# Score and value products of neighbouring maps issued in turns on the two halves of the tensor engine

## The chip, the cores and the metric

The kernel runs on one core of a Trainium2 chip. The metric is the device time of one execution in microseconds (us). A core has a tensor engine that does matrix products (PE; PEld is its weight load), a vector engine (DVE), a scalar engine (ACT), a general engine (POOL), and a sync engine (SP) whose queue starts most DMA transfers. All products here are fp32 or split fp32r; a plain fp32 product shows in the trace as two PE instructions.

## The reference

Two transformer blocks on 256 tokens of width 1024. The first mixes a gated delta rule (4 heads of 128, chunks of 64, a triangular solve) with a sliding "dilated" softmax attention (8 heads of 64), then has a dense gated feed-forward layer. The second has two layers, each with an attention and a mixture of 16 experts (top 2 of one group of 4). Layer one's attention is differential: 8 heads, each with two softmax maps of head size 64,

```
s = einsum('bqhmd,bkhmd->bmhqk', qb, k) + bias
p = softmax(where(allowed, s, NEG_INF))
a = p[:, 0] - lam_full * p[:, 1]
o = einsum('bhqk,bkhe->bqhe', a, v)
```

Layer two's attention is chunked: 16 heads of 64, one map each. So there are 8 + 16 + 16 = 40 maps of 256 queries by 256 keys. All are causal by blocks of 128: queries 128 to 255 see all 256 keys, queries 0 to 127 only the first 128.

## The kernel before, in words

**Layout.** The queries and keys of two heads (or of the two maps of one differential head) lie one above the other in the partitions: the tile `qT[:, blk, :]` has the features of one in partitions 0 to 63 and of the other in 64 to 127. A score product contracts over 64 partitions and so uses half of the rows of the tensor engine; the other half is free for the other map. A value product of `plain_heads` has 64 value features as stationary columns and contracts over 128 keys; it uses half of the columns, and writes its head's half of the partitions of the result.

**One map.** `scores` takes one PSUM tile and makes two products into it (lines 631 and 632, four PE instructions), then a fused add and minimum on DVE for each of the two query blocks (634, 636), two exponentials with sums on ACT (638, 639), and a reciprocal (640). The caller scales the rows (664, 665). `flip` transposes the map by three PE transposes (645 to 647) and copies it out (224 or 230, ACT and DVE in turns). `pv` makes the two value products of a head (653, 654, four PE instructions). After the odd head `split` writes the two halves of an fp32r number (ACT, then DVE, line 234).

**Stages and order.** `plain_heads` runs its heads through `lag`: step i issues the scores of head i, the flip of head i-2 and the value products of head i-3. It is used in three places: for the 8 dilated heads, whose steps `fill` drops between the steps of the delta rule (145 to 182 us of the span), and for four groups of 4 chunked heads (820 to 905 us). `diff_heads` does the same for the 8 differential heads, both maps of a head in one step (460 to 515 us). In the two attentions `weave` issues the steps of the first heads between the projections of the second half (`half(1)`, lines 586 to 588), and the steps of the later heads between the output projection (`proj(0)`, the same lines). The framework's planner takes the instructions in this order and sets the order on each engine by their readiness under its own costs, unless a line keeps them in program order. On the chip every engine takes its instructions in that order.

**Slots.** PSUM tiles of `ps` come from four slots (`pb`) and four more (`pa`, accumulators). SBUF tiles of `w2` (ten slots) hold the maps, the flipped maps and, in `half(1)`, the squares and normalised rows of the queries and keys (`unit_rows`). The expert weights are loaded by SP into ring slots and into tiles that the attention gives back (`wpair`, line 295; `v` among them).

Of the kernel before, what the change touches and what calls it, by code (L numbers as in the profile page):

```python
# [170 lines left out]
def tile_block(ctx: ExitStack, tc: tile.TileContext, a: dict, out: bass.AP, dbg=None):  # L171
# [11 lines left out]
    mm = nc.tensor.matmul  # L183
# [15 lines left out]
    def w2(shape, name, dt=F32):  # L199
        return act.tile([128] + shape, dt, tag="w2", name=name, bufs=10)  # L200
# [4 lines left out]
    def s1(w, name, bufs=2):  # L205
        return sm.tile([128, w], F32, tag=name, name=name, bufs=bufs)

    def ps(n=512, tag="pb"):
        p = pa if tag == "pa" else pb
        return p.tile([128, n], F32, tag=tag, name=tag)  # L210
# [21 lines left out]
    def split(h, l, i, eng=None):  # L232

        return A_.copy(h, i), (eng or V).tensor_tensor(l, i, h.bitcast(F32), op=ALU.subtract)  # L234

    def split_scaled(h, l, i, scale):
        return (A_.activation(h, i, AF.Copy, scale=scale),
                V.scalar_tensor_tensor(l, i, scale, h.bitcast(F32), op0=ALU.mult, op1=ALU.subtract))
# [231 lines left out]
    def rsq(o, i, scale):  # L470

        A_.activation(o, i, AF.Ln, bias=epsc, scale=scale)
        A_.activation(o, o, AF.Exp, scale=-0.5)
# [58 lines left out]
    def spread(rs):  # L532

        r = w2([S], "rows")
        for b in range(T):
            p = ps(128, "pa")
            mm(p, rs[:, b:b + 1].to_broadcast([128, 128]), ident, start=True, stop=True)
            V.tensor_copy(r[:, b * 128:(b + 1) * 128], p)
        return r
# [77 lines left out]
    def lag(n, *stages):  # L617

        for i in range(n + len(stages) - 1):
            for j, f in enumerate(stages):  # L620
                if 0 <= i - j < n:
                    f(i - j)
            yield


    def scores(qT, kT, blk, half, nbias, pt, den):


        h0 = half * 64
        p = ps(384)  # L630
        mm(p[:, 0:256], qT[h0:h0 + 64, blk, 128:256], kT[h0:h0 + 64, blk, :], start=True, stop=True)
        mm(p[:, 256:384], qT[h0:h0 + 64, blk, 0:128], kT[h0:h0 + 64, blk, 0:128], start=True, stop=True)
        mn = s1(2, "mn", 4)
        V.tensor_tensor_reduce(out=pt[:, 0:256], in0=p[:, 0:256], in1=nbias[:, ::-1], scale=1.0, scalar=3e38,
                               op0=ALU.add, op1=ALU.min, accum_out=mn[:, 0:1])
        V.tensor_tensor_reduce(out=pt[:, 256:384], in0=p[:, 256:384], in1=nbias[:, 0:128][:, ::-1], scale=1.0, scalar=3e38,
                               op0=ALU.add, op1=ALU.min, accum_out=mn[:, 1:2])
        A_.activation(pt[:, 0:256], pt[:, 0:256], AF.Exp, bias=mn[:, 0:1], scale=-1.0, accum_out=den[:, 0:1])
        A_.activation(pt[:, 256:384], pt[:, 256:384], AF.Exp, bias=mn[:, 1:2], scale=-1.0, accum_out=den[:, 1:2])
        V.reciprocal(den, den)  # L640

    def flip(pt):

        p = ps(384)
        nc.tensor.transpose(p[:, 0:128], pt[:, 256:384], ident)
        nc.tensor.transpose(p[:, 128:256], pt[:, 0:128], ident)
        nc.tensor.transpose(p[:, 256:384], pt[:, 128:256], ident)
        t = w2([384], "ptT")
        evac(t, p)
        return t  # L650

    def pv(o, v0, v1, t):
        mm(o, v0, t[:, 0:256], start=True, stop=False)
        mm(o[:, 128:256], v1, t[:, 256:384], start=False, stop=True)

    def plain_heads(h0, n, qT, kT, v, nbias, y):

        pts, ts, os_ = {}, {}, {}

        def first(i):  # L660
            h = h0 + i
            pt, den = w2([384], "pt"), s1(2, "den", 4)
            scores(qT, kT, h // 2, h % 2, nbias(h), pt, den)
            V.tensor_scalar(pt[:, 0:256], pt[:, 0:256], den[:, 0:1], None, op0=ALU.mult)
            V.tensor_scalar(pt[:, 256:384], pt[:, 256:384], den[:, 1:2], None, op0=ALU.mult)
            pts[h] = pt

        def second(i):
            ts[h0 + i] = flip(pts.pop(h0 + i))

        def third(i):
            h = h0 + i
            if h % 2 == 0:
                os_[h // 2] = ps(256)
            o = os_[h // 2]
            pv(o[h % 2 * 64:h % 2 * 64 + 64, :], v[:, 0, h * 64:h * 64 + 64], v[:, 1, h * 64:h * 64 + 64], ts.pop(h))
            if h % 2:
                split(*y(h // 2), o)

        return lag(n, first, lambda i: None, second, third)  # L680

# [18 lines left out]
    def l2(shape, name):  # L700
        return l1p.tile([128] + shape, F32, tag="l2", name=name, bufs=5)
# [29 lines left out]
    y = [None, None]  # L731
# [20 lines left out]
    n = 0  # L752
# [64 lines left out]
    for u in range(6):  # L817
        for j, (wh, wl) in enumerate(subs(a["w_qkv"][u] if u else first_)):
            f = 2 * u + j
            p = ps(256, "pa")  # L820
            feat(p, hh, wh, wl)
            o = qkvT[f // 4][:, f % 4]
# [17 lines left out]
        if u % 2:  # L840
            o = qkvT[u // 2].rearrange("p f t -> p (f t)")
# [13 lines left out]
    for h in range(4):  # L855
# [5 lines left out]
        p = ps(512)  # L861
        mm(p, ones, sq.rearrange("p i t -> p (i t)"), start=True, stop=True)
        r = w2([2, S], "rsq")
# [7 lines left out]
    def k_(h, b):  # L871
        return kq[:, h, b, 0, :]

    def q_(h, b):
        return kq[:, h, b, 1, :]
# [4 lines left out]
    p = ps(512)  # L880
# [25 lines left out]
    for b in range(T):  # L906
        for h2 in range(2):
            p = ps(512).rearrange("p (h i t) -> p h i t", h=2, i=2)
            for i in range(2):
                h = 2 * h2 + i  # L910
                mm(p[:, i].rearrange("p i t -> p (i t)"), k_(h, b), kq[:, h, b].rearrange("p i t -> p (i t)"),
                   start=True, stop=True)
# [7 lines left out]
    for b in range(T):  # L920
        p = ps(512)
# [6 lines left out]
    p = ps(512)  # L928
# [7 lines left out]
    for lv in range(6):  # L936
        os_ = w2([8, 64], "os")
# [20 lines left out]
        n = 128 if lv < 5 else 64  # L958
# [20 lines left out]
    u0, S1, r1, v1 = (l2([4, 128], n) for n in ("u0", "S1", "r1", "v1"))  # L979
    oo = l4([T, 512], "oo")  # L980

    def four(f):
        p = ps(512)
        for h in range(4):
            lhsT, rhs = f(h)
            mm(p[:, h * 128:(h + 1) * 128], lhsT, rhs, start=True, stop=True)
        return p
# [8 lines left out]
    p = four(lambda h: (k_(h, 1), S1[:, h]))  # L996
# [3 lines left out]
    p = four(lambda h: (q_(h, 1), S1[:, h]))  # L1000
    for h in range(4):
        o = oo[:, 1, h * 128:(h + 1) * 128]
        evac(o, p[:, h * 128:(h + 1) * 128], eg[:, 4 + h:5 + h])
    evac(flat(v1), four(lambda h: (YF[:, 4 + h], r1[:, h])))
    p = four(lambda h: (aq[:, 4 + h], v1[:, h]))
# [18 lines left out]
    for b in range(T):  # L1024
        for h in range(4):
            o = oo[:, b, h * 128:(h + 1) * 128]
            V.scalar_tensor_tensor(o, o, rso[:, b * 4 + h:b * 4 + h + 1], sz[:, b, h * 128:(h + 1) * 128],
                                   op0=ALU.mult, op1=ALU.mult)
    for h2 in range(2):
        p = ps(512).rearrange("p (h t) -> p h t", h=2)  # L1030
# [43 lines left out]
    nb = []  # L1074
# [20 lines left out]
    for f in range(NFF):  # L1095
        rooms[0] = "s8" if 1 <= f < 21 else "s"
        p, pu = ps(S), ps(S)
        for q, (wh, wl) in zip((p, pu), subs(a["w_gu"][f], by=(V, G) if f == 0 else None, behind=cols_done if f in (1,) else None)):
            feat(q, hh, wh, wl)
        o = w2([S], "gate")  # L1100
# [62 lines left out]
    h = cols_split(tx, spread(rs[:, 2:4]), mod[0]["gs1"], mod[0]["sh1"])  # L1163
# [463 lines left out]
    def diff_heads(c, qT, kT, v, y):  # L1627
        pts, ts, ons = {}, {}, {}

        def first(i):  # L1630
            h = 4 * c + i
            ab, dens = [], []
            for j in range(2):
                pt, den = w2([384], "pt"), s1(2, "den", 4)
                scores(qT, kT, h, j, nb[c][:, i, :], pt, den)
                ab.append(pt)
                dens.append(den)
            V.tensor_scalar(dens[1], dens[1], nlam, None, op0=ALU.mult)
            for j, sl in enumerate((slice(0, 256), slice(256, 384))):
                V.tensor_scalar(ab[1][:, sl], ab[1][:, sl], dens[1][:, j:j + 1], None, op0=ALU.mult)  # L1640
                V.scalar_tensor_tensor(ab[0][:, sl], ab[0][:, sl], dens[0][:, j:j + 1], ab[1][:, sl],
                                       op0=ALU.mult, op1=ALU.add)
            pts[i] = ab[0]

        def second(i):
            ts[i] = flip(pts.pop(i))

        def third(i):
            h = 4 * c + i
            t = ts.pop(i)  # L1650
            o = ps(256).rearrange("p (b d) -> p b d", b=2)
            v0, v1 = v[:, 0, h * 128:(h + 1) * 128], v[:, 1, h * 128:(h + 1) * 128]
            mm(o[:, 0], t[:, 0:128], v0, start=True, stop=True)
            mm(o[:, 1], t[:, 128:256], v0, start=True, stop=False)
            mm(o[:, 1], t[:, 256:384], v1, start=False, stop=True)
            on, ss = w2([T, 128], "on"), s1(2, "oss", 4)
            for b in range(T):
                A_.activation(on[:, b], o[:, b], AF.Square, accum_out=ss[:, b:b + 1])
            rsq(ss, ss, 1.0 / 128)
            V.tensor_tensor(on, o, ss.unsqueeze(2).to_broadcast([128, T, 128]), op=ALU.mult)  # L1660
            ons[i] = on

        def fourth(i):
            on = ons.pop(i)
            p = ps(256)
            for b in range(T):
                nc.tensor.transpose(p[:, b * 128:(b + 1) * 128], on[:, b], ident)
            split_scaled(y[0][c][:, i], y[1][c][:, i], p, sub8)

        return lag(4, first, second, third, fourth)  # L1670

    def between():
# [21 lines left out]
    h = cols_split(tx[0], kept(spread(rs), 1), m_["gs1"], m_["sh1"])  # L1694

    nb = []
# [41 lines left out]
```

## Time and profile before

| | before |
|---|---|
| median of 3 runs | 1158.78 us (1157.76 to 1162.37) |
| profiled execution | 1160.73 us, span 1158.7 us |
| PE busy | 1103.9 us (95%) |
| PE weight load busy | 710.5 us (61%) |
| DVE busy | 595.2 us (51%) |
| ACT busy | 449.6 us (39%) |
| mean granted PE clock | 0.984 |
| DMA | 349.71 MB, mean 302 GB/s |

A matrix product's time in a row is from its start to its modelled end, and successive products overlap; the time that a product costs the engine is the distance from its start to the next one's. A row of the timeline merges successive products of one line: its start is the start of the first.

### The profile page before, as it was taken

What the parts mean: (1) busy time and instruction counts of PE and PEld (TensorE: products, weight loads), DVE (VectorE), ACT (ScalarE), POOL (GpSimd) and SP (SyncE); (2) the same over time, 40 slices, a digit from 0 to 9 for tenths busy, and PEclk for the clock granted to TensorE, in tenths of its full rate; (3) what the DMA queues carried; (4) which work ended last, traced back from release to release, by engine and by line L of the source; (5) the groups of instructions that cost most, each with busy time, mean ns of one, the idle gap of its engine ahead of it and who ended that gap; (6) DMA issues with size and microseconds to landing.
All of it is one profiled execution on the core that took longest, in us unless ns stands there. A gap on an engine that the chain in (4) does not pass through costs nothing. (4 is left out here: it accounts for less than half of the span.)

```text
span 1158.7 us, 16795 instructions
## 1 busy us (share of the span) xinstructions
PE 1103.9 (95%) x6524; PEld 710.5 (61%) x6524; DVE 595.2 (51%) x1211; ACT 449.6 (39%) x907; POOL 161.3 (14%) x132
## 2 busy tenths in 40 slices
PE   8999999999999989998999997999999899999798
PEld 6967766799898968785443433337776544343332
DVE  6954355798999666886231212126566713121212
ACT  5752254656555465775111102026555511110200
POOL 2223112132223141012000000003221100000000
PEclk9999999999999989999999999999999989999999
DMA  8686777878887945357798999997663779899994
GB/s 326 224 314 227 294 263 242 293 254 330 323 319 284 370 149 188 128 210 257 298 383 327 424 424 420 422 420 272 202 194 133 267 278 384 339 424 424 422 420 198
DMA packets 53007, 349.71 MB, mean 302 GB/s; under 512 B 6356, under 2 KB 7108, under 8 KB 12984
## 3 DMA queue, kind: packets, MB, share of 16 engines
q1 hardware_dynamic: 50288, 342.51, 75.9%
q0 software_dynamic: 1792, 5.62, 1.8%
q8 instruction: 54, 0.88, 0.3%
q10 hardware_dynamic: 840, 0.43, 0.1%
q14 instruction: 33, 0.27, 0.1%
HBM read 347.40 MB, written 1.14 MB: 301 GB/s over the span
## 5 line engine op out<-in xcount | busy, mean ns | idle before, releaser
L1571 PE MATMUL pb<-w,XT 128*64 128x512 f32 x864 | 200.4, 613 | 10.1 <-PEq L1531 10.1
L234 ACT CAST wh<-w 128x1024 fp32r<-128x1024 f32 x132 | 137.7, 1044 | 100.8 <-PE pa L587 74.0
L234 DVE TENSOR_TENSOR wl<-w,wh 128x1024 fp32r<-128x1024 f32 x110 | 135.2, 1230 | 58.5 <-ACT wh L234 49.5
L1571 PEld LDWEIGHTS pb<-w,XT 128*64 128x64 f32 x864 | 61.7, 140 | 127.8 <-issue 123.3
L1608 PE MATMUL pb<-w,heT 128*64 128x512 f32 x480 | 108.1, 596 | 1.5 <-ACT heT L224 1.5
L1590 DVE TENSOR_TENSOR he<-he,pb 128x512 f32<-128x512 f32 (+1 forms) x20 | 11.4, 581 | 175.4 <-PE pb L1571 175.4
L586 PE MATMUL pa<-wh,hh 128*128 128x512 f32 x224 | 91.6, 410 | 2.5 <-ACT hh L559 2.5
L587 PE MATMUL pa<-wh,hl 128*128 128x512 f32 x224 | 89.7, 400 | 3.0 <-POOL hl L557 1.7
L1589 ACT ACTIVATE he<-pb 128x512 f32<-128x512 f32 (+1 forms) x20 | 10.0, 512 | 207.7 <-PE pb L1571 207.7
L588 PE MATMUL pa<-wl,hh 128*128 128x512 f32 x224 | 89.3, 399 | 0.0
L234 POOL TENSOR_TENSOR wl<-w,wh 128x1024 fp32r<-128x1024 f32 x22 | 53.0, 2408 | 248.5 <-ACT wh L234 197.2
L1611 DVE SCALAR_TENSOR_TENSOR he<-pb,gsl,g 128x512 f32<-128x512 f32 x32 | 24.0, 751 | 96.9 <-PE pb L1608 96.8
L1608 PEld LDWEIGHTS pb<-w,heT 128*64 128x64 f32 x480 | 32.7, 137 | 64.6 <-issue 58.6
L570 PE MATMUL pb<-hh,whl 128*128 128x256 f32 x320 | 61.9, 286 | 0.0
L383 POOL TENSOR_TENSOR acc<-acc,wa 128x512 f32<-128x512 f32 x24 | 41.4, 1724 | 125.9 <-DVE acc L385 90.9
L234 ACT CAST yh<-he 128x512 fp32r<-128x512 f32 x30 | 18.5, 617 | 103.6 <-DVE he L1611 103.6
L570 PE MATMUL pb<-hh,wh 128*128 128x256 f32 x192 | 54.4, 284 | 0.0
L570 PE MATMUL pb<-hl,wh 128*128 128x256 f32 x192 | 54.3, 283 | 0.0
L570 PE MATMUL pb<-hh,wl 128*128 128x256 f32 x192 | 54.3, 283 | 0.0
L570 PEld LDWEIGHTS pb<-hh,whl 128*128 128x128 f32 x320 | 51.2, 191 | 2.3 <-issue 1.8
L587 PEld LDWEIGHTS pa<-wh,hl 128*128 128x128 f32 x224 | 43.3, 193 | 12.5 <-DVE hl L560 2.2
L586 PEld LDWEIGHTS pa<-wh,hh 128*128 128x128 f32 x224 | 42.8, 192 | 12.8 <-ACT hh L559 3.4
(459 smaller groups left out, 2317.5 us busy)
## 6 DMA issues: line engine op xcount, KB each, us to landing
w<-in_m_gu SPq DMA_DIRECT2D x108, 1024.0 KB, 10.8
w<-in_m_dn SPq DMA_DIRECT2D x58, 1024.0 KB, 9.0
wa<-in_ada_p SPq DMA_DIRECT2D x24, 1024.0 KB, 5.0
wa<-in_ada_w SPq DMA_DIRECT2D x24, 1024.0 KB, 5.0
w<-in_w_gu SPq DMA_DIRECT2D x22, 1024.0 KB, 6.9
w<-in_a_qkv SPq DMA_DIRECT2D x12, 1024.0 KB, 12.4
wx<-in_m_gu SPq DMA_DIRECT2D x12, 1024.0 KB, 5.9
w<-in_b_qkv SPq DMA_DIRECT2D x12, 1024.0 KB, 14.8
```

The lines of the kernel that those rows point to most:

```text
L234: return A_.copy(h, i), (eng or V).tensor_tensor(l, i, h.bitcast(F32), op=ALU.subtract)
L383: G.tensor_tensor(acc, acc, wi, op=ALU.add)
L570: mm(p, w[:, c], r[:, k, :], start=(n == 0), stop=(n == 3 * KD - 1))
L586: mm(p[b], hh_, wh[:, c], start=(k == k0), stop=False)
L587: mm(p[b], hl_, wh[:, c], start=False, stop=False)
L588: mm(p[b], hh_, wl[:, c], start=False, stop=((k + 1) % KD == k0))
L1571: mm(pu[i][64 * e:64 * e + 64, :], xt[k // 4][:, k % 4, c0 + 64 * e:c0 + 64 * e + 64], w(e, i), start=(k == 0), stop=(k == KD - 1))
L1589: A_.activation(he[:, cs], pu[0][:, cs], AF.Silu)
L1590: V.tensor_tensor(he[:, cs], he[:, cs], pu[1][:, cs], op=ALU.mult)
L1608: pin(mm(pd[h][64 * e:64 * e + 64, :], heT[:, k, e, :], w(e, i), start=(k == 0), stop=(k == 3)))
L1611: V.scalar_tensor_tensor(he, pd[h], gsl, g2[:, h * 512:(h + 1) * 512], op0=ALU.mult, op1=ALU.mult)
```

## The change

`scores` is cut in two. `maps` makes the score products of both halves, product by product in turns, into two PSUM tiles; `softmaxed` does what followed for one of them. `plain_heads` calls `maps` at the even head for itself and the odd one, keeps both PSUM tiles, and the odd head's step only does the softmax. Its value products are made at the odd head for both heads in turns, so that the even head's step makes none; the flipped map of the even head is kept a step longer, and the PSUM tile of the result is taken a step later. `diff_heads` calls `maps` once for its two maps. Lines, sizes, and the number of all instructions are otherwise the same; no DMA is moved.

```
-    def scores(qT, kT, blk, half, nbias, pt, den):
-        h0 = half * 64
-        p = ps(384)
-        mm(p[:, 0:256], qT[h0:h0 + 64, blk, 128:256], kT[h0:h0 + 64, blk, :], start=True, stop=True)
-        mm(p[:, 256:384], qT[h0:h0 + 64, blk, 0:128], kT[h0:h0 + 64, blk, 0:128], start=True, stop=True)
+    def maps(qT, kT, blk):
+        p = [ps(384), ps(384)]
+        for o, q, n in ((slice(0, 256), slice(128, 256), 256), (slice(256, 384), slice(0, 128), 128)):
+            for half in range(2):
+                r = slice(half * 64, half * 64 + 64)
+                mm(p[half][:, o], qT[r, blk, q], kT[r, blk, 0:n], start=True, stop=True)
+        return p
+
+    def softmaxed(p, nbias, pt, den):
...
-    def pv(o, v0, v1, t):
-        mm(o, v0, t[:, 0:256], start=True, stop=False)
-        mm(o[:, 128:256], v1, t[:, 256:384], start=False, stop=True)
...
         def first(i):
+            q = h0 // 2 + i // 2
+            if i % 2 == 0:
+                done[q] = maps(qT, kT, q)
             h = h0 + i
             pt, den = w2([384], "pt"), s1(2, "den", 4)
-            scores(qT, kT, h // 2, h % 2, nbias(h), pt, den)
+            softmaxed(done[q][i % 2], nbias(h), pt, den)
...
         def third(i):
-            h = h0 + i
-            if h % 2 == 0:
-                os_[h // 2] = ps(256)
-            o = os_[h // 2]
-            pv(o[h % 2 * 64:h % 2 * 64 + 64, :], v[:, 0, h * 64:h * 64 + 64], v[:, 1, h * 64:h * 64 + 64], ts.pop(h))
-            if h % 2:
-                split(*y(h // 2), o)
+            if i % 2 == 0:
+                return
+            h, o = h0 + i - 1, ps(256)
+            for b, t, c in ((0, slice(0, 256), slice(0, 256)), (1, slice(256, 384), slice(128, 256))):
+                for j in range(2):
+                    mm(o[64 * j:64 * j + 64, c], v[:, b, (h + j) * 64:(h + j) * 64 + 64], ts[h + j][:, t], start=(b == 0), stop=(b == 1))
+            split(*y(h // 2), o)
...
+            p = maps(qT, kT, h)
             for j in range(2):
                 pt, den = w2([384], "pt"), s1(2, "den", 4)
-                scores(qT, kT, h, j, nb[c][:, i, :], pt, den)
+                softmaxed(p[j], nb[c][:, i, :], pt, den)
```

## Rows read from the trace of the kernel before

**Rows 1.** Stages: start:end, length, busy us of each engine, clock, DMA share, GB/s.

```profile
core 0: us, PE busy (x) PEld busy (x) DVE busy (x) ACT busy (x) POOL busy (x), PEclk, DMA share, GB/s
163.50:182.00 18.50, 18.50 (x94) 11.35 (x94) 11.58 (x50) 8.38 (x35) 5.92 (x9) 1.00 0.77 258
815.00:865.00 50.00, 50.00 (x235) 39.07 (x233) 29.89 (x57) 26.05 (x51) 9.83 (x13) 1.00 0.62 188
865.00:905.00 40.00, 39.60 (x200) 26.63 (x200) 26.97 (x106) 23.51 (x69) 3.46 (x3) 1.00 0.35 131
```

**Rows 2.** PE's waits from 815 to 905 us: total, times, longest.

```profile
PE pb L645 <- DVE den L640: 0.3, 1, 0.3
```

**Rows 3.** Timeline of PE, chunked attention: start, us, line, out<-in, shape, count.

```profile
841.23 0.39 PE L587 MATMUL pa<-wh,hl 128*128 128x512 f32 x1
841.45 0.39 PE L588 MATMUL pa<-wl,hh 128*128 128x512 f32 x1
841.77 0.70 PE L631 MATMUL pb<-kT,qT 64*128 64x256 f32 x2
842.31 0.38 PE L632 MATMUL pb<-kT,qT 64*128 64x128 f32 x2
842.62 0.33 PE L645 MATMUL pb<-ident,pt 128*128 128x128 f32 x1
...
844.16 0.40 PE L588 MATMUL pa<-wl,hh 128*128 128x512 f32 x1
844.49 0.65 PE L653 MATMUL pb<-ptT,v 128*64 128x256 f32 x2
844.97 0.38 PE L654 MATMUL pb<-ptT,v 128*64 128x128 f32 x2
845.28 0.50 PE L586 MATMUL pa<-wh,hh 128*128 128x512 f32 x1
845.62 0.39 PE L587 MATMUL pa<-wh,hl 128*128 128x512 f32 x1
```

**Rows 4.** Timeline of PE, differential attention, one head's two maps.

```profile
460.27 0.71 PE L631 MATMUL pb<-kT,qT 64*128 64x256 f32 x4
460.81 0.40 PE L632 MATMUL pb<-kT,qT 64*128 64x128 f32 x4
461.13 0.50 PE L586 MATMUL pa<-wh,hh 128*128 128x512 f32 x1
```

**Rows 5.** Timeline of PE, differential attention, the heads that stand otherwise.

```profile
504.67 0.71 PE L631 MATMUL pb<-kT,qT 64*128 64x256 f32 x4
505.20 0.39 PE L632 MATMUL pb<-kT,qT 64*128 64x128 f32 x4
505.42 0.59 PE L631 MATMUL pb<-kT,qT 64*128 64x256 f32 x2
...
506.17 0.50 PE L586 MATMUL pa<-wh,y 128*128 128x512 f32 x1
```

**Rows 6.** Timeline of PE, chunked attention, three maps around a value product.

```profile
879.00 0.70 PE L631 MATMUL pb<-kT,qT 64*128 64x256 f32 x2
879.62 0.65 PE L653 MATMUL pb<-ptT,v 128*64 128x256 f32 x2
...
880.42 0.37 PE L632 MATMUL pb<-kT,qT 64*128 64x128 f32 x1
880.42 0.48 PE L631 MATMUL pb<-kT,qT 64*128 64x256 f32 x1
...
881.49 0.50 PE L587 MATMUL pa<-wh,y 128*128 128x512 f32 x1
```

**Rows 7.** Groups of PE's products by line and shape: count, busy us, mean ns.

```profile
L1571 PE MATMUL pb<-w,XT 128*64 128x512 f32 x864 | 200.4, 613 | 10.1 <-PEq L1531 10.1
```

**Rows 8.** Timeline of PE, the dilated heads; in brackets idle time and its releaser.

```profile
148.52 1.02 PE L975 MATMUL pb<-R,X 64*64 64x64 f32 x14
150.46 1.06 PE L399 MATMUL pa<-wa,csil 128*32 128x512 f32 x8 [0.92 <-DMA wa<-in_ada_p]
...
171.95 0.70 PE L631 MATMUL pb<-kb,qb 64*128 64x256 f32 x2
...
172.80 0.33 PE L645 MATMUL pb<-ident,pt 128*128 128x128 f32 x1
...
173.28 0.65 PE L653 MATMUL pb<-ptT,vb 128*64 128x256 f32 x2
...
174.07 0.70 PE L631 MATMUL pb<-kb,qb 64*128 64x256 f32 x2
```

**Rows 9.** Groups of DVE, 865 to 905 us: count, busy us, mean ns.

```profile
L634 DVE CUSTOM_DVE_ANT_0 pt<-pb,nb 128x256 f32<-128x256 f32 x12 | 5.0, 418 | 5.1 <-POOL wl L234 2.2 <-PE pb L632 1.7 <-issue 1.2
L664 DVE TENSOR_SCALAR pt<-pt,den 128x256 f32<-128x256 f32 x12 | 4.2, 352 | 0.2
L636 DVE CUSTOM_DVE_ANT_0 pt<-pb,nb 128x128 f32<-128x128 f32 x12 | 3.4, 284 | 0.0
L665 DVE TENSOR_SCALAR pt<-pt,den 128x128 f32<-128x128 f32 x12 | 3.4, 282 | 0.0
L230 DVE COPY ptT<-pb 128x384 f32<-128x384 f32 x6 | 3.3, 552 | 1.3 <-PE pb L647 1.3
L234 DVE TENSOR_TENSOR y<-pb,y 128x256 fp32r<-128x256 f32 x6 | 2.5, 422 | 3.1 <-ACT y L234 3.1
L640 DVE RECIPROCAL den<-den 128x2 f32<-128x2 f32 x12 | 2.0, 165 | 1.4 <-ACT pt L639 1.3
```

**Rows 10.** The SP queue's waits, 866 to 935 us: total, times, longest.

```profile
SPq L295 <- PE pb L654: 30.8, 1, 30.8
```

**Rows 11.** PE's waits, 930 to 1150 us (the last experts), the longest two.

```profile
PE pb L1597 <- DVE he L1590: 5.0, 7, 0.9
PE pb L1571 <- PEq L1531: 5.0, 1, 5.0
```

**Rows 12.** Weight loads of the value products: duration min/median/max in ns.

```profile
L653 PEld LDWEIGHTS pb<-ptT,v x32: 132/134/137, 844.5 to 903.9; 128*64 128x64 f32 x32
```

**Rows 13.** Timeline of PE, score products of two successive rounds of `weave`.

```profile
828.44 0.70 PE L631 MATMUL pb<-kT,qT 64*128 64x256 f32 x2
...
834.97 0.70 PE L631 MATMUL pb<-kT,qT 64*128 64x256 f32 x2
```

More of the change, by code (lines that the diff above doesn't have):

```diff
@@ L650, in flip @@
         return t
-    def pv(o, v0, v1, t):
-        mm(o, v0, t[:, 0:256], start=True, stop=False)
-        mm(o[:, 128:256], v1, t[:, 256:384], start=False, stop=True)
     def plain_heads(h0, n, qT, kT, v, nbias, y):
-        pts, ts, os_ = {}, {}, {}
+        pts, ts, done = {}, {}, {}
         def first(i):
+            q = h0 // 2 + i // 2
+            if i % 2 == 0:
+                done[q] = maps(qT, kT, q)
             h = h0 + i
             pt, den = w2([384], "pt"), s1(2, "den", 4)
-            scores(qT, kT, h // 2, h % 2, nbias(h), pt, den)
+            softmaxed(done[q][i % 2], nbias(h), pt, den)
             V.tensor_scalar(pt[:, 0:256], pt[:, 0:256], den[:, 0:1], None, op0=ALU.mult)
```

## The prediction

> **What bounds the kernel now.** I read the busy times by stage first, then PE's waits, then the timeline of PE around the changed lines. In the three stages that hold the changed products PE is busy for 18.50 of 18.50, 50.00 of 50.00 and 39.60 of 40.00 us [rows 1]; from 815 to 905 us it waits 0.3 us in all [rows 2]. A busy PE is not yet a PE at its peak, so the starts must be looked at: the plain 512-column products beside a map start every 0.22 to 0.23 us (841.23, 841.45), without a gap [rows 3]. So time taken off PE here is time off the span, as long as DVE and ACT keep up: DVE is busy 11.6 of 18.5 us, 29.9 of 50 and 27.0 of 40 [rows 1].
>
> **The price of a map and of a value product now.** A map alone, between 841.77 and the next start at 842.62, costs 0.85 us [rows 3]; it also comes 0.32 us after the start of the product before it (841.45) instead of 0.23, and a 512-column product that follows a half-array product takes 0.34 us to the next start (845.28 to 845.62) instead of 0.23: 0.2 us for going to half an array and back. A value product costs 0.79 us (844.49 to 845.28) and the same 0.2 us around it [rows 3].
>
> What two maps side by side cost is in the same trace: in the differential attention both maps of a head show as one run, four first and then four second instructions, from 460.27 to 461.13, 0.86 us [rows 4]. So the kernel before, though written map by map, already runs two maps at once there, because they stand next to each other in PE's order and use different rows. That is the main thing to see: what the change brings is less the turns than that heads which stood steps apart come to stand together. For two value products on the two halves of the columns the nearest row is the expert product on 64 columns, in turns: 200.4 us for 864 instructions of 512 columns is 0.23 us each [rows 7], and a map's 256-column instruction alone takes about 0.22 (842.31 less 841.77, less some 0.1 us of first load, halved) [rows 3]: twice the columns in the same time, so the halves run fully beside each other. I take 0.80 us for a pair, bounded by that and by two alone (1.59).
>
> **The change part by part.**
>
> Differential heads: of eight pairs six stand as in rows 4; the other two make a run of three maps in 1.50 us (504.67 to 506.17) [rows 5] and a map alone, 0.85 [rows 3]. After: 2 x 0.86. That is 2.35 - 1.72 = 0.6 us, and one switch less, 0.1: 0.7 us. Bounds 0 and 1.
>
> Chunked heads, 815 to 865 us: four maps and four value products, each alone between projection products. Two merges of maps at 0.84 + 0.2 and two of value products at 0.78 + 0.2 give 4.0 us. DVE has 20 us free in that stage [rows 1], and the projections cover any late softmax: taken whole.
>
> Chunked heads, 865 to 905 us: twelve maps, twelve value products. Some maps stand together already: a run of three as in rows 5, a pair as in rows 4, and three that cost 0.62 + 1.07 = 1.69 us around a value product [rows 6]; with four alone that makes 1.50 + 0.86 + 1.69 + 3.40 = 7.45 us, against 6 x 0.86 = 5.16: 2.3 us. Six merges of value products are 6 x 0.78 = 4.7, and some nine half-array runs fewer at about 0.1 each 0.9. Sum 7.9 us. But here DVE's 27.0 us would stand in 32 instead of 40. A head costs DVE 0.42 + 0.28 + 0.35 + 0.28 + 0.17 + half of 0.55 + half of 0.42 = 2.0 us [rows 9], and PE 0.43 + 0.48 + 0.40 = 1.3 after the change (0.48 is the flip, 172.80 to 173.28 [rows 8]). Only the output projection between the heads keeps PE the slower one. I take 5.7 of 7.9, nearer to the whole since PE waited 0.3 us before; bounds 0 and 7.9.
>
> Dilated heads: eight maps and eight value products, each alone [rows 8]: 4 x 0.84 + 4 x 0.78 = 6.5 us of PE. Three of the maps lie before 163 us between steps of the delta rule, where PE is already waiting now (from the end of line 975 at 149.5 to 150.46) [rows 8]: a map less there gains nothing. From 163.5 us on the heads follow each other without a gap, but with DVE at 11.6 us in what would be 13. I take 3.5; bounds 0 and 6.5.
>
> What hides the rest. The odd map's softmax now comes a step after its scores, and the even head's value product a step later; PE has flips, the other pair and projections to do in between. The queue behind a late flip is PE's own: everything stands in one order. SP's queue waits 30.8 us for the last value product (line 654) to give `v` back, then loads the expert weights [rows 10]. That product comes earlier with the stage, so the loads move with it, and in the last experts PE's longest waits are for DVE and its own queue, none for a load [rows 11]: the lead is kept and what the attentions save reaches the end.
>
> The sum: 0.7 + 4.0 + 5.7 + 3.5 = 13.9 us of 19.1 on PE. The profiled execution took 1160.73 us, so 1146.8; the median is 1.95 us under it, so **1144.8, said as 1145 us**.
>
> **A rule against the change.** The two weight loads of a value product take 0.134 us each [rows 12], and within one value product they cost little, since the second load runs beside the first product (844.49 to 844.97 is 0.48 us for two products of 0.21 and one load) [rows 3]. The Trainium skill, "TensorE: Matmul & The Clock Gate", section "Part 3: Packing small matmuls — row/col tiling", says that a weight load overlaps products in flight only when its row group differs, and that products never pass each other. The maps differ in rows, the value products do not, and by that rule the latter would gain less; the trace bears it out poorly, as the expert products share all rows and run at 0.23 us. As a mechanism of this kernel: if the four loads of the second head stood free, a pair would cost 0.79 + 4 x 0.134 = 1.33 us instead of 0.80, 12 x 0.53 = 6.4 us less on PE, about 4.5 of it on the path: 1149.5 us.
>
> **The rivals.**
>
> A. DVE and the odd head's softmax set the pace where heads follow heads. For it: 2.0 against 1.3 us a head [rows 9], and the planner may place flips too early if it counts two maps one after the other. Against: 0.3 us of waits now [rows 2], and projections to put between. It would leave 0.7 + 4.0 + 2 = 6.7 us: 1152.
>
> B. The value products do not run beside each other as the expert products do; the case above, 1149.5 us.
>
> C. The planner parts what was put together, or the plan elsewhere shifts by as much as is won: 1158.
>
> D. Slower, by the ten `w2` slots. A flipped map is now kept a step longer: three maps and three flipped maps instead of three and two, beside the squares and rows of `unit_rows` (up to two and four) while `half(1)` is woven in: eleven or twelve for ten slots. Where a row tile waits for a slot, its projection accumulator is not read, and PE, in order, stands until the next value pair, up to a round of `weave`, 6.5 us (828.44 to 834.97) [rows 13]. The two calls have four such tiles. It decides from three lost rounds on, 19.6 us against 13.9: 1164. Against it: PE shows no such wait now, though the slots must be near full.
>
> **How the numbers follow.** The forecast has 0.60, its own range 1139 (all 19.1) to 1151 (only 8). A has 0.17, B 0.06, C 0.08, D 0.09. Half a per cent, about what a measurement here can tell from no change, is 5.8 us: 1153.0 and 1164.6. Faster: the forecast, B and 0.12 of A, 0.78. Same: 0.05 of A, C, and 0.01 of D: 0.14. Slower: the rest of D, 0.08. The range reaches from 1138 (19.1 and a microsecond or two of an earlier delta rule) to 1160, so that it takes in A, B and C and leaves out D and a little below.
>
> **What would show it.** The maps of the dilated and chunked heads as runs of four and four in 0.86 us, 20 in all; twelve value runs of four and four in 0.80; the differential stage within 1 us of before; the stage from 815 to 865 us shorter by 4 and the next by 5 to 8; waits of PE for DVE at the flips of the chunked heads of at most 2 or 3 us. A value pair of 1.3 us would show B, waits of several us at flips A, waits of ACT line 1180 or PE line 586 for a slot D. I am wrong if PE's products take as little as said and the span keeps the time all the same.

## The result, and the profile after

After: 1144.99 us, median of 4 runs (1143.55 to 1146.97); before, on the same chip, 1158.49 us, 4 runs (1157.76 to 1162.37). The ratio is 0.9878, 95% interval 0.9863 to 0.9893: faster by 13.5 us, where 13.9 had been forecast. The same kernel, measured again later (e10 below), gave 1144.63 us and 0.9879. The profiled execution took 1144.52 us.

The totals of the page after; PE's busy time is 14.2 us less, DVE's and ACT's 3.0 and 1.8.

```profile
span 1142.6 us, 16798 instructions
PE 1089.7 (95%) x6524; PEld 701.6 (61%) x6524; DVE 592.2 (52%) x1211; ACT 447.8 (39%) x907; POOL 161.2 (14%) x132
```

To compare stages, both traces are cut at the same instructions: from the delta rule's last product of line 986 to the last transpose behind the dilated heads; from the first differential map to the end of the output projection; from the first chunked map to the end of its output projection. The columns are those of [rows 1]. Before:

```profile
163.43:183.66 20.23, 20.23 (x105) 12.77 (x103) 12.52 (x53) 9.43 (x37) 5.92 (x9) 1.00 0.76 249
460.27:538.34 78.07, 77.32 (x420) 62.96 (x420) 59.74 (x179) 54.90 (x170) 8.38 (x5) 1.00 0.52 188
821.90:914.11 92.21, 91.81 (x447) 67.78 (x446) 58.06 (x167) 50.18 (x127) 12.32 (x13) 1.00 0.50 173
```

The same stages after:

```profile
162.50:177.22 14.72, 14.72 (x99) 9.20 (x97) 12.58 (x53) 9.66 (x37) 5.91 (x9) 1.00 0.93 292
452.98:531.82 78.84, 77.54 (x421) 63.06 (x420) 59.95 (x179) 54.13 (x170) 8.38 (x5) 1.00 0.52 185
815.61:898.85 83.24, 82.74 (x446) 63.52 (x446) 57.31 (x167) 49.58 (x127) 12.26 (x13) 1.00 0.54 185
```

By these lengths the stages take 5.5 us less, 0.8 more and 9.0 less, 13.7 less in all. PE is still busy nearly throughout, and the granted clock stays 1.00, so what went is work of PE and neither a wait nor the clock.

The differential and the chunked cuts hold the same products before and after. The dilated cut does not: after, one map stands ahead of it, beside its partner (at 152.69 us), and two projection products have moved behind its end. Carried on to the last product of that projection, the stretch is, before and then after,

```profile
163.43:205.95 42.52, 42.17 (x203) 28.42 (x202) 22.40 (x66) 18.36 (x48) 8.29 (x10) 1.00 0.76 271
162.50:200.01 37.51, 37.15 (x199) 25.23 (x198) 22.15 (x66) 18.10 (x48) 8.29 (x10) 1.00 0.91 306
```

5.0 us less instead of 5.5. With that the three stages come to 13.2 us.

PE's timeline after, columns as in [rows 3]: a pair of maps and a pair of value products that stand whole, then two that do not.

```profile
498.03 1.57 PE L633 MATMUL pb<-kT,qT 64*128 64x256 f32 x12
499.53 0.50 PE L586 MATMUL pa<-wh,y 128*128 128x512 f32 x1
...
500.47 0.92 PE L633 MATMUL pb<-kT,qT 64*128 64x256 f32 x4 [0.21 <-DVE y L238]
501.32 0.50 PE L588 MATMUL pa<-wl,y 128*128 128x512 f32 x1
...
815.61 0.92 PE L633 MATMUL pb<-kT,qT 64*128 64x256 f32 x8
816.46 0.50 PE L586 MATMUL pa<-wh,hh 128*128 128x512 f32 x1
...
854.67 0.87 PE L683 MATMUL pb<-ptT,v 128*64 128x256 f32 x8
855.47 1.57 PE L633 MATMUL pb<-kT,qT 64*128 64x256 f32 x12
...
863.41 0.65 PE L683 MATMUL pb<-ptT,v 128*64 128x256 f32 x2
863.98 0.50 PE L588 MATMUL pa<-wl,y 128*128 128x512 f32 x1
...
865.11 0.87 PE L683 MATMUL pb<-ptT,v 128*64 128x256 f32 x6
865.91 0.50 PE L586 MATMUL pa<-wh,y 128*128 128x512 f32 x1
```

A whole pair of maps costs 0.85 us (815.61 to 816.46), a whole pair of value products 0.80 (854.67 to 855.47). At 863.41 the first two instructions of a value pair stand alone, with projection products behind them, and the other six come later: 0.57 + 0.80 us. Of twelve value pairs eight are whole and four are parted like this. Two map pairs at 498.03 likewise come as twelve and four instructions: one of the four score tiles (`pb`) was still being read by DVE (line 238, in `split_scaled`).

PE's waits from 815 to 891 us after; they answer to [rows 2].

```profile
PE pb L651 <- ACT pt L645: 0.3, 1, 0.3
PE pb L633 <- DVE y L234: 0.2, 1, 0.2
```

Half a microsecond: nothing took the place of the work that went. In the last experts the waits are those of [rows 11] again (line numbers have moved by 6):

```profile
PE pb L1577 <- PEq L1537: 5.3, 1, 5.3
PE pb L1603 <- DVE he L1596: 5.0, 7, 0.9
```

### The profile page after: what moved, and what is told of

The parts are those of the page before. It is cut to its first block, busy times and chain, and to the rows that moved or that the text cites. A ratio compares the mean times of both kernels' runs of the same rounds, so it can differ in the third digit from the quotient of the medians.

```text
span 1142.6 us, 16798 instructions
## 1 busy us (share of the span) xinstructions
PE 1089.7 (95%) x6524; PEld 701.6 (61%) x6524; DVE 592.2 (52%) x1211; ACT 447.8 (39%) x907; POOL 161.2 (14%) x132
## 5 line engine op out<-in xcount | busy, mean ns | idle before, releaser
L1596 DVE TENSOR_TENSOR he<-he,pb 128x512 f32<-128x512 f32 (+1 forms) x20 | 11.4, 580 | 175.4 <-PE pb L1577 175.3
```

What stands on the lines that cost most here:

```text
L1596: V.tensor_tensor(he[:, cs], he[:, cs], pu[1][:, cs], op=ALU.mult)
```

## The experiments

Medians are of each kernel's own runs; "before" is the kernel before on the same chip. Lengths of the three stages (cut as above) are given as dilated / differential / chunked, against before's 20.2 / 78.1 / 92.2 us.

**e1, adjacent but map by map.** What the pairs' neighbourhood is worth without the turns.

```
-        for o, q, n in (...):
-            for half in range(2):
+        for half in range(2):
+            for o, q, n in (...):
...
-            for b, t, c in (...):
-                for j in range(2):
+            for j in range(2):
+                for b, t, c in (...):
```

> Both heads' maps are issued at the even head and both heads' value products at the odd head as in the kernel after, but map by map and head by head, not in turns. Theory (what counts is that two maps stand next to each other in PE's order; the engine itself starts the second on the free half): 1146 us (1144 to 1149), run of two maps 0.86 us; about 1 us above the kernel after because value pairs that the planner parts lose all of their overlap instead of half. Rival (the turns are what makes the halves run together): 20 maps cost 0.85 us more each, 1158 us or more.

Measured: 1150.39 us against 1157.95, ratio 0.9935 (0.9912 to 0.9959). By the median alone 5 us would belong to the turns. By the stages, 15.0 / 78.1 / 84.4 (the same products in each cut as after the change), the neighbourhood alone brings 13.0 us of the change's 13.7. A pair is as short as with turns:

```profile
815.09 0.93 PE L633 MATMUL pb<-kT,qT 64*128 64x256 f32 x8
815.95 0.50 PE L586 MATMUL pa<-wh,hh 128*128 128x512 f32 x1
```

0.86 us. The 5 us are lost far from the change, at the experts' branch; e7 to e9 take that up.

**e2, the differential heads alone.** `diff_heads` calls `maps`; everything else as before.

> Only the differential heads get their maps in turns; the plain heads are issued as in the kernel before. Theory (those pairs overlapped already): 1157.5 to 1158.5, no change that can be told. Rival (each of the eight pairs is halved): 8 x 0.85 = 6.8 us, 1151.7.

Measured: 1159.95 us against 1157.95, ratio 1.0016 (1.0004 to 1.0029). Stages 20.2 / 78.6 / 92.2: this part of the change costs 0.6 us where it acts. What it costs there is taken up below, with the prediction.

**e3, the maps alone,** and **e4, the value products alone.** Each takes one half of the change; the other products stay head by head as before.

> The maps as in the kernel after, the value products head by head as before. Theory (PE bounds these stages and the two parts add up): the maps' 3.4 + 0.7 + 4 us of PE less what is not passed on: 1152 (1149.5 to 1154). Rival (after one half another engine bounds the stage, so that either part alone brings nearly all): 1146 to 1148.

> The value products as in the kernel after, the maps map by map at their own heads as before. Theory (PE bounds, the parts add up): 9 to 10 us of PE less the pairs that the planner parts: 1151 (1149 to 1153); its gain and that of the maps alone add up to the 13.5 of both. Rival (another engine bounds after one part): 1146 to 1148. Rival (value pairs share their rows, so their loads do not overlap): 1155.

Measured: e3 1151.25 us, ratio 0.9956 (0.9942 to 0.997), stages 19.2 / 78.5 / 87.0; e4 1153.7 us, ratio 0.9965 (0.9946 to 0.9984), stages 16.7 / 78.1 / 87.3. The two gains by stages are 5.8 and 8.4 us, 14.2 together against 13.7 of the whole: the halves add up to within half a microsecond. (Their dilated cuts do not hold quite the same products, e3's six more of line 399, e4's three fewer of the projection, so this is good to about a microsecond.) By the medians they come to 11.0 only; e4 has a like loss at the branch as e1.

**e5, both maps on the same half of the rows.** The maps stay neighbours in turns, but nothing can overlap. Left out: the scores of every odd map, in whose place stand those of the even one.

```
-                r = slice(half * 64, half * 64 + 64)
+                r = slice(0, 64)
```

> The kernel after, but both maps of a pair take the lower 64 partitions (the scores of the second map are those of the first head, left as they are): same instructions, same order, same slots, no free half. Theory (the gain of the maps is the overlap of the two halves): 20 x 0.85 = 17 us more than the kernel after, 1162 (1157 to 1164), a run of two maps 1.5 to 1.7 us. Rival (the gain comes from the new order and the slots): 1145.

Other scores send tokens to other experts, and the branch for an overfull expert runs (its products of line 1281 alone keep PE busy for 493.2 us): the whole time, 2109.15 us, can't be compared, the stages can: 15.5 / 81.1 / 86.2. A pair is now

```profile
818.73 1.57 PE L633 MATMUL pb<-kT,qT 64*128 64x256 f32 x8
820.23 0.50 PE L586 MATMUL pa<-wh,hh 128*128 128x512 f32 x1
```

1.50 us. So of the 0.85 us that a second map costs when it stands alone, 0.65 go by the overlap on the two halves, and 0.2 by standing next to the first. The stages are 6.0 us longer than after, less than the theory's 17. That counted 0.85 us for each of the 20 pairs, where a whole pair loses 0.65 and those that were late or parted after the change lose less. All map products together, start to next start, take 30.04 us on PE against 20.81 after, 9.2 more. Of these 1.2 belong to two pairs ahead of the dilated cut, and PE's idle time in the stages, 1.8 us after and none here, takes up another part.

**e6, value pairs held together.** The even head's first value product is ordered behind the odd head's first, so that the planner can't set it earlier.

```
-                for j in range(2):
-                    mm(o[64 * j:64 * j + 64, c], ...)
+                for j in ((0, 1) if b else (1, 0)):
+                    i_ = mm(o[64 * j:64 * j + 64, c], ...)
+                    if b == 0 and j:
+                        lead = i_.ins.name
+                    elif b == 0:
+                        after(i_, lead)
```

> The kernel after with the even head's first value product ordered behind the odd head's first one, so that the four value pairs that the planner parts stay whole. Theory (PE bounds: a parted pair costs 0.58 + 0.79 us and one more change of the array's halves, a whole one 0.80): 4 x 0.75 = 3 us less, 1142 (1141 to 1144). Rival (the early product fills a gap that PE would have waited in anyway): 1145.

Measured: 1142.69 us against 1158.8, ratio 0.9863 (0.9837 to 0.989). All twelve value pairs are whole, as the timeline of the stretch that was parted at 863 us shows:

```profile
862.75 0.87 PE L683 MATMUL pb<-ptT,v 128*64 128x256 f32 x8
863.55 0.33 PE L651 MATMUL pb<-ident,pt 128*128 128x128 f32 x1
...
864.93 0.87 PE L683 MATMUL pb<-ptT,v 128*64 128x256 f32 x8
865.73 1.93 PE L633 MATMUL pb<-kT,qT 64*128 64x256 f32 x16
```

and the chunked stage loses 2.4 us more than with the change (80.84 against 83.24; columns as above):

```profile
162.86:177.80 14.94, 14.94 (x103) 9.78 (x102) 13.21 (x54) 9.67 (x37) 5.91 (x9) 1.00 0.83 265
451.11:529.70 78.59, 77.55 (x421) 63.04 (x420) 59.97 (x179) 54.11 (x170) 8.37 (x5) 1.00 0.51 186
813.56:894.40 80.84, 80.40 (x446) 62.31 (x446) 56.96 (x167) 48.40 (x123) 11.82 (x13) 1.00 0.55 188
```

**e7, e8, e9: the same work, other places in the code.** In e1 and e4 PE stands at the overflow branch of the last experts for 10.4 and 9.0 us, after the change for 5.3. The traces count 12751 PE instructions ahead of the branch's target after the change, 12749 in e1 and in e4 (other orders need two semaphore waits fewer). Counted are the products, weight loads and semaphore instructions recorded ahead of the first weight load behind the branch. Warm-up products at the very start, whose results nobody uses, shift the code by four instructions each time: one more in e1 (e7) and e4 (e9), one fewer in the changed kernel (e8).

```
-    for _ in range(5):
+    for _ in range(6):     # e7, e9; range(4) in e8
```

> The kernel of e1_by_map (score products adjacent but map by map, value products adjacent but head by head) with 6 instead of 5 warm-up products at the start, which puts every later instruction of TensorE 4 places further on (12753 instead of 12749 instructions ahead of the target of the last experts' branch). Theory (e1's 5 us against the change come from a second fetch of code at that branch, which hangs on the place of the code): TensorE's gap at the branch falls from 10.4 back to about 5.2 us with one instruction fetch in it, and the time is 1145 to 1147 us. Rival (issuing by turns is itself worth 5 us): the time stays at 1150 us.

> The changed kernel with 4 instead of 5 warm-up products, so that its code stands 4 places earlier (12747 instead of 12751 instructions). Theory of the code's place: the second fetch comes in here too, the gap at the branch is about 10 us, and the time is about 1150 us. Rival (the second fetch belongs to the order by map): 1145 us.

> The kernel of e4_values_only (value products by turns, score products as before the change) with 6 warm-up products (12753 instead of 12749 instructions). Theory of the code's place: the gap at the branch falls from 9.4 to about 5.2 us and the time from 1153.7 to about 1149.5 us, so that the gains of the score products alone and of the value products alone, where neither holds a second fetch, come within 2 us of adding up to the whole. Rival: it stays at 1153.7 us.

> The changed kernel, unaltered, on the same chip as the three shifted kernels: 1145 us, the gap at the branch 5.2 us. It is the base for them, and says how far one chip differs from the next.

Measured, before at 1157.73 us: e7 1145.78 (ratio 0.9884, 0.9864 to 0.9904), e8 1146.74 (0.9911, 0.9896 to 0.9926), e9 1148.14 (0.9915, 0.9902 to 0.9927), e10 1144.63 (0.9879, 0.986 to 0.9899). The stages stay as they were (e7 15.0 / 78.1 / 84.4 as e1; e9 16.7 / 78.1 / 87.3 as e4; e10 as after). PE's wait at the branch, e1:

```profile
PE pb L1577 <- DMA w<-in_m_dn: 10.4, 1, 10.4
```

e7, where two fetches of code now run side by side:

```profile
PE pb L1577 <- PEq L1537: 6.8, 1, 6.8
```

e8, the changed kernel with one warm-up product fewer:

```profile
PE pb L1577 <- DMA w<-in_m_dn: 10.4, 1, 10.4
```

and e9:

```profile
PE pb L1580 <- PEq L1540: 5.1, 1, 5.1
```

The wait moves with the place of the code and not with the order of the products: it comes to the changed kernel in e8 and leaves the by-map order in e7 and the value half in e9. So e1's and e4's medians carried a loss that is no part of the change, and the rival, that the turns are worth 5 us, falls: e7 and e10 differ by 1.15 us, within their runs (1140.99 to 1149.21 and 1139.72 to 1146.02). Three things came out otherwise than expected. e7's wait fell to 6.8 and not to 5.2 us. And e8's median rose by 2.1 us only: its profiled run, at 1150.08, is one of two near 1150, the other three are near 1146.6; why those are shorter the one profile can't tell. Nor do the medians of the halves add up now: e3 is 6.7 us and e9 9.6 under before, 16.3 together, 2.8 more than the whole, where less than 2 had been expected. That the halves add up thus rests on the stages alone.

**e11, value pairs held together and the differential maps as before.**

```
-            p = maps(qT, kT, h)
...
-                softmaxed(p[j], nb[c][:, i, :], pt, den)
+                softmaxed(one_map(qT, kT, h, j), nb[c][:, i, :], pt, den)
```

> The kernel of e6_values_kept (all value pairs held together), with the differential attention's score products put back as they were before the change, each head's second map behind its first map's softmax. Theory (in the differential stage, where the planner had already set the two maps of a head side by side, issuing by turns only makes the second map wait in the first one's way where its accumulator is not yet free): the differential stage, +0.5 us against before in e6, goes back to 0, the chunk keeps its -11.4 us and the dilated attention its -5.3, and the time is about 0.5 to 0.8 us below e6's on the same chip, so about 1142 us, provided that the branch in the last experts shows one fetch of code (a gap of 5.2 us); with a second fetch it would be up to 5 us more. Rival (the differential stage gains by the turns too): slower than e6 by 1 to 4 us.

**e12, e6 again.**

> The kernel of e6_values_kept, unaltered, on the same chip as e11. Theory (pairs that the planner cannot part keep 2.3 us more of the chunk than the change does): 1142.5 us, a ratio to before of 0.986, against 0.988 of the change on three chips. Rival (the first run was a lucky chip): 1145 us, ratio 0.988.

Measured, before at 1158.08 us: e11 1144.89 (0.988, 0.9856 to 0.9903), e12 1141.48 (0.9859, 0.9837 to 0.9881). The stages of e11, columns as above:

```profile
164.18:179.12 14.94, 14.94 (x103) 9.80 (x102) 13.20 (x54) 9.67 (x37) 5.91 (x9) 1.00 0.80 265
452.59:530.65 78.06, 77.31 (x421) 62.98 (x420) 59.74 (x179) 54.88 (x170) 8.38 (x5) 1.00 0.52 187
811.98:892.84 80.86, 80.42 (x447) 62.33 (x446) 56.94 (x167) 48.43 (x123) 11.82 (x13) 1.00 0.54 187
```

The differential stage is back at before's 78.06, as the theory said; e12's is 78.58. But e11 counts 12749 instructions ahead of the branch, and PE's wait there is

```profile
PE pb L1587 <- DMA w<-in_m_dn: 10.5, 1, 10.5
```

so the 0.5 us won in the attention were paid back tenfold in the last experts. e6 is the fastest kernel that was run: 1142.69 and 1141.48 us on two chips against 1144.99 and 1144.63 of the change (measured twice; the three chips of the expectation are not on record). The intervals of the ratios overlap; that e6 is the shorter rests on the 2.4 us of the chunked stage, which both its profiles show to 0.03 us.

## Why the prediction was right

The time came out as forecast, 1144.99 against 1145 us, and the mechanism is the one named: heads that stood apart now stand together, and the turns as such add 0.7 us of 13.7 (after against e1, by stages), none that the medians of e7 and e10 can tell. That the sum came so close is partly luck. For the same work the stages give 13.2 us where 13.9 had been forecast, and the terms' errors cancelled: the differential heads came out 1.5 us worse than forecast, the chunked 0.7 worse, the dilated 1.5 better.

- *Prices.* Forecast 0.86 us for a pair of maps and 0.80 for a pair of value products; measured 0.85 and 0.80 where a pair stands whole. The sign given, 20 map pairs and twelve value pairs at these prices, came in part: eleven map pairs take 0.85 to 0.92 us, the other nine, late or parted, 1.26 on average, and four of the value pairs are parted. The reading of [rows 4], that PE runs two maps at once although they are issued one after the other, holds: e1's pair takes 0.86, e5's on one half 1.50.
- *Differential heads, forecast 0.7 us less.* The step that failed: it took all eight pairs as whole after the change and put no wait of PE beside them. The heads of [rows 5] are parted after as before (498.03: twelve and four), since what parts them is a score tile not yet free and not the order in which they are issued. (Of the six pairs that it took at 0.86 us before, two take 0.89 and 1.01.) And PE waits longer for DVE behind the fourth head, at a value product and at a transposition. Before, and then after:

```profile
PE pb L1653 <- DVE on L1660: 0.5, 1, 0.5
...
PE pb L1660 <- DVE on L1667: 0.8, 1, 0.8
PE pb L651 <- DVE pt L1648: 0.3, 1, 0.3
```

PE's idle time in the stage rows goes from 0.75 to 1.30 us, which is most of the 0.8 us that the stage is longer. The rest goes with the last pair, at 508.02, whose second map starts 0.4 us behind the first; it takes 1.25 us instead of 1.01. In e2, where nothing else is changed, the value product waits 0.8 us and the last pair takes 1.25 too, and the stage is 0.6 us longer; in e1 and e11, issued map by map, all three are as before. Why DVE comes later behind maps in turns is open.

- *Chunked heads, forecast 4.0 + 5.7 = 9.7 us less.* Measured 9.0. The full sum was 4.0 + 7.9 = 11.9; it was cut to 9.7 for fear of DVE, which was the wrong reason: PE waited 0.5 us. What kept the rest is the planner (C, in small): three parted value pairs and the parted map pairs. With the value pairs held together (6.41 us of PE instead of 8.36, the maps unchanged at 8.60) e6's stage is 11.4 us shorter than before, nearly the full sum.
- *Dilated heads, forecast 3.5 of 6.5.* Mis-sized: 5.5 by the cut, 5.0 for the same work. PE stays busy for all of the 14.72 us; DVE, with 12.58 us in them, kept up. The map that moved ahead of the cut costs nothing there: two pairs take 1.77 us of PE where three maps took 2.70.
- *Loads keep their lead.* Right: after, SP's longest wait from 850 to 930 us is again for the last value product, 26.8 us where it was 30.8 [rows 10], and no PE wait for a weight appears in the last experts.

```profile
SPq L295 <- PE pb L683: 26.8, 1, 26.8
```

- *The rivals.* A: no flip waited more than 0.3 us. D: no wait for a `w2` slot. B: the value pair would have had to cost 1.33 us. The Trainium skill, "TensorE: Matmul & The Clock Gate", section "Part 3: Packing small matmuls — row/col tiling", lets a weight load overlap products in flight only where the row group differs; the trace does not agree for two halves of the columns, where the second head's loads cost the pair 0.01 us over one head alone (0.80 against 0.79, [rows 3]). Nor do the runs bear out the other half of that sentence of the prediction, that products never pass each other: two maps on different halves of the rows do, as the last section shows.
- *The rest.* The profiled spans differ by 16.1 us, the stages by 13.2 for the same work. In e10 the same stages are the same to 0.02 us and the span is 4.1 us shorter still (1138.5): what lies between the attentions varies by some microseconds from one execution to the next, so the other 2.9 can't be put down to the change.

## What to carry to other kernels

Before pairing half-array products, look for a place where two already stand next to each other: its length is the price of a pair, and the gain is to be counted by pairs that the schedule will in fact leave whole, not by all pairs; one ordering edge that keeps the pairs whole took 2.4 us more off a stage. Cut the traces at the same instructions, see by the counts that the cuts hold the same work, and compare stages: here they repeated to some hundredths of a microsecond while the whole times moved by several. And where a median disagrees with the stages, look at what the whole program does elsewhere, such as its branches.

## What the runs showed of the hardware that had not been expected

**PE fills a free row half by itself.** Issued map by map, the second map's products start beside the first's, and issuing them in turns adds next to nothing. It is not the planner that sets them in turns: in its program of the kernel before, lines 631 and 632 of one map stand ahead of 631 and 632 of the other, and [rows 4] shows all four instructions of line 631 ahead of those of line 632. So the statement above that every engine takes its instructions in the planner's order does not hold for PE's products on different halves of the rows.

**A branch can cost a second fetch of code, by the place of its target.** At the branch PE stands while a 16 KB instruction transfer brings the code: in most kernels the transfer starts 2.5 to 2.7 us after the start of PE's last product (from which all times here count), some 2.5 us later PE's next semaphore instruction shows, and the next such transfer starts 5.6 to 6.0 us behind the first. In e1 and e11 (12749 instructions ahead of the target) PE gets through the first of the three semaphore instructions ahead of the weight load at 5.03 us, and the next comes at 10.6; in e8 (12747) it gets through all three, at 5.11, 5.26 and 5.43, and the weight load comes at 10.82. So each of them stops behind the 12747th recorded instruction, which puts the edge of the fetched block there; with 12750 and more ahead, all three lie behind the edge. The kernels with that many (before, after, e2, e6, e9, e10 and e12) go on at 5.4 to 5.6 us; all four below it (e1, e4, e8, e11) wait for a second fetch, until 9.4 (e4) or 10.8 to 10.9 us. In e3 and e7, above the edge, two transfers start within 0.3 us of each other and PE goes on at 7.2 us; why they do so is open. The row names the weights' DMA as the releaser. But in e1 and e8 SP starts the weights' transfers at the same distances ahead of PE's last product as after the change, the latest 4.0 us ahead, and there PE goes on at 5.6 us; so the weights are not what it waits for. Two semaphore waits more or fewer, which any reordering can bring, thus decide about 5 us in the profile of this kernel.
